# Where the memory's matrices of a hybrid encoder layer are computed: at the start, or in turns with later work

## The chip, the cores and the metric

The kernel runs on one core of a Trainium2 chip. The core has a matrix engine (TensorE, PE in the profile), whose weight loads the profile keeps apart (PEld), a vector engine (VectorE, DVE), a scalar engine (ScalarE, ACT), GpSimd (POOL) and SyncE (SP). Each engine works through its own list of instructions in order; semaphores order the engines against each other. Transfers are started by an instruction on SP, ACT or POOL and run on 16 DMA engines. The metric is device time in microseconds (us) of one execution; smaller is better.

## The reference

One encoder layer over x (2048 tokens of 1024) with a memory of 256 rows:

```python
y = rmsnorm(h, norm_mix_g) @ w_in          # q, k, v, and the conv's value and gate
att = dilated_sliding_attention(q, k, v)   # three patterns, strides 1, 4 and 16
u = a * sigmoid(g)                         # the gated units
conv = silu(layernorm(depthwise_conv(u)))
h = h + concat(att, conv) @ w_out

xq = rmsnorm(h, norm_x_g) @ w_xq           # 4 heads of 256
mn = rmsnorm(mem, norm_mem_g)
xk, xv = mn @ w_xk, mn @ w_xv
pr = softmax(xq xk^T / 16);  h = h + (pr xv) @ w_xo

h = h + square(relu(rmsnorm(h, norm_mlp_g) @ w_up)) @ w_down
return rmsnorm(h, norm_final_g)
```

The cross attention's weights depend on the memory alone. The kernel therefore works out two products per head once, ahead of their use: a score matrix w_xq xk^T (called `pa` in PSUM, `ea` when evicted, `ascr` in DRAM) and a back matrix xv w_xo (`pb`, `eb`, `bscr`).

## The kernel before, in words

The program is one long stream of PE work. Generators stand for the parts; `weave` advances several by given rates, and `pinned` keeps a part's instructions behind what was emitted before them on one engine. What is left open is placed by a scheduler, so the order on each engine is not just that of the code. `ps(kind, ...)` takes a PSUM bank of a kind in turn; `banks` says which banks a kind has, and it is changed between stages.

Products that need float32 accuracy are made of three matmuls on high and low parts (`mm3`, L263 to L266): high by high, low by high, high by low. A weight arrives as `raw`, ACT copies its high part, and DVE or POOL subtracts to get the low one (`wsplit2` L252, `scaled_split` L219).

The stages, in the profile's time:

1. *Start, 0 to 107 us* (`setup0` L148, `setup`, `memory` L414, `xprep` L388). `memory` transposes the memory rows (`mt`), projects the keys with w_xk (`proj` L463: 8 groups of 24 matmuls, `pxk`), transposes w_xq (`turned_wq` L481: 16 groups of 4 transposes, `xqt`, each evicted by an ACT copy and a DVE subtraction) and computes the 16 score groups of 12 matmuls (`pa`, L505 on). It takes turns with `xprep(0)` and `xprep(1)`: squares on ACT for the norm, transposes `xt`, and the high and low parts `xh` (ACT) and `xl` (POOL) of the first 1024 tokens, 512 at a time.
2. *Gated units and projections, 107 to about 455 us*: `pipeline` L604 runs `glu` L624 (two units of 24 matmuls per 512 tokens and 128 channels) for tokens 0 to 1023, then `lin_qk` and `lin_v`; `xprep(2)` and `xprep(3)` lie beside it. The first gated matmul is the first `lin`.
3. *Far stretch, about 455 to 700 us*: attention with stride 16 (`att_far` L983, 124 steps), woven with a filler L1241: the gated units of the later 1024 tokens in turn with `values` L517, which projects the values with w_xv (`pxv`, 8 groups of 24 matmuls) and makes the back matrices (`pb`, 16 groups of 6 matmuls of 512 columns, evicted by ACT at L577).
4. *The rest*: `post` L1453 for four groups of 512 tokens, which begins with `load_cat` L1318, 14 transfers on SP that bring the operand `cath`, `catl` of w_out, and its matmuls `o`; then cross attention and the MLP.

Of the kernel before, what the change touches and what calls it, by code (L numbers as in the profile page):

```python
# [47 lines left out]
def hybrid_layer(ctx, tc, A, out):  # L48
# [16 lines left out]
    banks = {"mm": (0, 1, 2), "a": (3, 4), "b": (5, 6), "c": (7,), "mem": "b"}  # L65
# [17 lines left out]
    def pinned(gen, *names):  # L83

        while True:
            with ExitStack() as st:
                after(st, *names)
                if next(gen, st) is st:
                    return
            yield  # L90

# [27 lines left out]
    vscr = dr.tile([2, KC, P, NMEM], F32R, name="vscr")  # L119
# [28 lines left out]
    def setup0():  # L148
        mvec = t2("mvec", F32, (8, P))
        dma(mvec, A["norm_mem_g"][0].rearrange("(k p) -> k p", p=P))  # L150
        pm = ps("c", "pmvec")
        PE.transpose(pm[:, 0:8], mvec, ident[0:8, 0:8])
        ACT.copy(gm, pm[:, 0:8])

    def setup():
# [7 lines left out]
        dma(vecs[GV["final"]:GV["final"] + 8, :], A["norm_final_g"].rearrange("(k p) -> k p", p=P))  # L163
        dma(cwn[0:CW, :], A["conv_w"][0])
# [197 lines left out]
    def load_nat(sp, src, name, bufs=10, q=None):  # L362
# [9 lines left out]
    def sumsq(sp, t, ss, j, n):  # L372

        for e in range(2):
            q = sp.tile([P, 512], BF16, tag="junk", name="junk", bufs=1)
            ACT.activation(q, t[e], AF.Square, accum_out=ss[:, n * e + j:n * e + j + 1])
# [11 lines left out]
    def xprep(sp, n):  # L388
        xtiles(n)
        nat = [load_nat(sp, A["x"][0, 512 * n + P * j:512 * n + P * (j + 1), :], f"xn{n}_{j}", q=nc.gpsimd if n else None) for j in range(4)]  # L390
# [6 lines left out]
        for k in range(KC):  # L397
# [8 lines left out]
            ACT.copy(XH_[k, n], xv)  # L406
# [7 lines left out]
    def memory(sp, mp):  # L414

        def mpool(part, i, n, name, shape, dtype=F32R):
            return mp.tile(list(shape), dtype, tag=f"m{n}{part}{i}", name=name)

        nat = [load_nat(sp, A["mem"][0, P * j:P * (j + 1), :], f"mn{j}") for j in range(2)]
        mh, ml = ([mpool(q, i, 3, f"m{q}{i}", (P, 4, NMEM)) for i in range(2)] for q in "hl")  # L420
        for k2 in range(KC // 2):
            pt = ps("b", f"mt{k2}")
# [4 lines left out]
            for e in range(2):  # L427
# [4 lines left out]
                DVE.scalar_tensor_tensor(lv, src, gain("mem", k), f(hv), op0=ALU.mult, op1=ALU.subtract)  # L432
        for i, t in enumerate((*mh, *ml)):
            dma(f(mscr[i]), f(t), nc.gpsimd)
        r = rstd_nat(sp, nat, "m")
        rb = ps("c", "rbm")
        bcast_rows(rb, r, 2)
        DVE.tensor_copy(rmem[:, 0:2], r[:, 0:2])
        rbm = sp.tile([P, 2, NMEM], F32, tag="rbm", name="rbm")
        for q in range(2):  # L440
            ACT.activation(rbm[:, q], rb[:, 0:NMEM], AF.Copy, scale=-1.0 / 16.0)
        yield
        cnt = [0]

        def wtiles(name, shape=(P, 8, P)):
            i = cnt[0]
            cnt[0] += 1
            if i % 5 < 2:
                raw = wp.tile(list(shape), F32, tag="raw", name=f"mraw_{name}", bufs=2)
            else:  # L450
                raw = lp.tile(list(shape), F32, tag="lraw", name=f"mraw_{name}", bufs=3)
            if i % 3 < 2:
                return [raw] + [wp.tile(list(shape), F32R, tag=t, name=f"m{t}_{name}", bufs=2) for t in ("whi", "wlo")]
            return [raw] + [mpool(q, 0, 2, f"m{q}_{name}", shape) for q in "hl"]

        def split(src, name, shape=(P, 8, P)):
            raw, hi, lo = wtiles(name, shape)
            dma(raw, src)
            ACT.copy(hi, raw)
            DVE.tensor_tensor(lo, raw, f(hi), op=ALU.subtract)  # L460
            return hi, lo

        def proj(w, name, th, tl):  # L463

            for j in range(KC):
                wh, wl = split(wcols(w, j * P), f"{name}{j}")
                pt = ps("mm", f"p{name}{j}")[:, 0:256]
                for k in range(KC):
                    mm3(pt, wh[:, k, :], wl[:, k, :], mh[k // 4][:, k % 4, :], ml[k // 4][:, k % 4, :],
                        k == 0, k == KC - 1)  # L470
                hv, lv = th[j // 4][:, j % 4, :], tl[j // 4][:, j % 4, :]
                ACT.copy(hv, pt)
                DVE.tensor_tensor(lv, pt, f(hv), op=ALU.subtract)
                yield

        def ttiles(name):
            return [[mpool(q, 2 + i, 3, f"t{q}{name}{i}", (P, 4, NMEM)) for i in range(2)] for q in "hl"]

        th, tl = ttiles("k")
        yield from proj(w_xk, "xk", th, tl)  # L480
        def turned_wq(h):  # L481
            wt = []
            for e in range(2):
                j = 2 * h + e
                raw, whi, wlo = wtiles(f"xq{j}")
                dma(raw, wcols(w_xq, j * P))
                for g in range(2):
                    pt = ps("b", f"xqt{j}{g}")
                    for i in range(4):
                        PE.transpose(pt[:, i * P:(i + 1) * P], raw[:, 4 * g + i, :], ident)  # L490
# [1447 lines left out]
```

## Time and profile before

| what | us |
|---|---|
| median of 3 runs (2831.89, 2821.95, 2821.16) | 2821.95 |
| the profiled execution's own time | 2819.71 |
| its span, first to last instruction | 2817.9 |
| PE busy | 2701.2 |
| DVE, ACT, POOL busy | 1893.7, 1271.2, 510.1 |
| mean granted TensorE clock | .983 |

The profiled execution is one run with a profile taken. Its span leaves out 1.8 us around the first and the last instruction. Busy times overlap between engines and between neighbouring matmuls: a busy PE can still be waiting inside its pipeline, so the prediction counts matmuls by the distance from one start to the next. A row of a group reads: line, engine, operation, output and input names, shapes, count, busy time, mean ns of one, and after the last bar the idle time of the engine ahead of them with what ended it. A row of the timeline reads: start, duration, engine, line, names, and in brackets the idle time before and its releaser.

### The profile page before, as it was taken

To read this page: it belongs to the slowest core of one execution; us is meant where nothing else is said; L and a number is where in the kernel's file an instruction comes from. 1 tells how busy PE (TensorE), PEld (TensorE's weight loads), DVE (VectorE), ACT (ScalarE), POOL (GpSimd) and SP (SyncE) were. 2 spreads that over 40 slices of the span, in tenths; PEclk is the share of its full clock that TensorE was granted. 3 is DMA by queue.
4 is the path that set the end of the run, shared out by engine and by line. 5 is a ranking of instruction groups with operands and counts; after the bars stand their busy time and mean duration, and the time that the engine had idled before them with its cause. 6 is when DMAs were issued, how large, how long until landed. Compare 5 with 4: busy or idle time off the path is not lost.

```text
span 2817.9 us, 40543 instructions
## 1 busy us (share of the span) xinstructions
PE 2701.2 (96%) x14783; PEld 2083.1 (74%) x14783; DVE 1893.7 (67%) x3475; ACT 1271.2 (45%) x2172; POOL 510.1 (18%) x700
## 2 busy tenths in 40 slices
PE   7899999898799999999999999999999999999998
PEld 7554445666677887787878788878887788878877
DVE  5456872665588875667987478766475786666665
ACT  5564322766344333434554443454344444444435
POOL 3346421232002122300111201121010121200000
PEclk8999999999899999999999999999999999999999
DMA  8875555696635666767467866774544554584553
GB/s 283 245 192 135 123 140 162 178 240 187 207 108 172 207 212 222 235 219 219 126 188 222 258 203 213 234 237 139 172 127 131 176 194 154 183 292 155 166 183 105
DMA packets 495135, 531.47 MB, mean 189 GB/s; under 512 B 81253, under 2 KB 371673, under 8 KB 494936
## 3 DMA queue, kind: packets, MB, share of 16 engines
q1 hardware_dynamic: 467528, 440.27, 52.3%
q0 software_dynamic: 25680, 85.38, 8.3%
q10 hardware_dynamic: 1728, 3.24, 0.3%
q8 instruction: 116, 1.90, 0.3%
q14 instruction: 83, 0.68, 0.1%
HBM read 382.36 MB, written 146.42 MB: 188 GB/s over the span
## 4 chain that ended last, share of the span: by engine, by line
PE 69%; DMA 9%; issue 8%; DVE 7%; ACT 3%; POOL 2%; SPq 1%; POOLq 0%; ACTq 0%; DVEq 0%
PE b L1636 7%; PE dn L264 4%; PE dn L265 4%; PE dn L266 4%; PE up L264 3%; PE up L266 3%; PE up L265 3%; PE lin L264 3%; PE lin L265 3%; PE lin L266 3%; PE pt L940 2%; PE s L1133 2%; PE xs L264 1%; PE xs L266 1%; PE xs L265 1%
## 5 line engine op out<-in xcount | busy, mean ns | idle before, releaser
L281 DVE SCALAR_TENSOR_TENSOR cacc<-cu,cwu,cacc 128x512 f32<-128x512 f32 x480 | 390.8, 816 | 6.3
L264 PE MATMUL dn<-hhh,whi_d 128*128 128x512 f32 x512 | 201.7, 404 | 4.3 <-ACT hhh L1473 2.6
L264 PE MATMUL up<-mh,whi_u 128*128 128x512 f32 x512 | 203.9, 398 | 0.0
L934 ACT ACTIVATE sm<-sm,o 128x256 f32<-128x256 f32 (+1 forms) x384 | 160.0, 466 | 96.7 <-DVE o L933 96.3
L265 PE MATMUL dn<-hhl,whi_d 128*128 128x512 f32 x512 | 199.8, 393 | 0.8 <-DVE hhl L1474 0.8
L266 PE MATMUL up<-mh,wlo_u 128*128 128x512 f32 x512 | 200.0, 391 | 0.0
L265 PE MATMUL up<-ml,whi_u 128*128 128x512 f32 x512 | 199.7, 390 | 0.0
L266 PE MATMUL dn<-hhh,wlo_d 128*128 128x512 f32 x512 | 198.8, 391 | 0.0
L933 DVE CUSTOM_DVE_ANT_0 sm<-s,mask 128x256 f32<-128x256 f32 (+1 forms) x384 | 127.2, 374 | 61.3 <-PE s L1133 35.1
L944 DVE TENSOR_TENSOR pl<-pt,ph 128x512 f16<-128x512 f32 x160 | 109.3, 685 | 56.6 <-ACT ph L943 56.4
L1488 DVE TENSOR_TENSOR h<-h,dn 128x512 f32<-128x512 f32 x128 | 86.3, 683 | 70.9 <-PE dn L266 70.4
L943 ACT CAST ph<-pt 128x512 f16<-128x512 f32 x160 | 92.2, 577 | 85.6 <-PE pt L940 85.3
L242 POOL TENSOR_TENSOR nr<-st_v,mhalf 128x4 f32<-128x4 f32 x12 | 13.5, 1125 | 627.8 <-DVE st_v L238 627.8
L264 PE MATMUL o<-cath,whi_o 128*128 128x512 f32 x256 | 103.6, 406 | 12.3 <-DMA cath<-cath 10.8
L264 PEld LDWEIGHTS dn<-hhh,whi_d 128*128 128x128 f32 x512 | 95.4, 188 | 23.3 <-ACT hhh L1473 3.7
L266 PEld LDWEIGHTS up<-mh,wlo_u 128*128 128x128 f32 x512 | 96.1, 188 | 20.4
L266 PEld LDWEIGHTS dn<-hhh,wlo_d 128*128 128x128 f32 x512 | 96.2, 188 | 20.2
L265 PEld LDWEIGHTS dn<-hhl,whi_d 128*128 128x128 f32 x512 | 96.3, 188 | 19.3 <-DVE hhl L1474 1.5
L940 PE MATMUL pt<-ident,sm 128*128 128x128 f32 x640 | 100.9, 277 | 9.8 <-DVE pl L944 3.6
L265 PEld LDWEIGHTS up<-ml,whi_u 128*128 128x128 f32 x512 | 96.3, 188 | 18.7
L264 PEld LDWEIGHTS up<-mh,whi_u 128*128 128x128 f32 x512 | 96.2, 188 | 18.6
L264 PE MATMUL x<-pth,whi_b 128*128 128x512 f32 x256 | 100.3, 397 | 2.4 <-ACT xp L1394 1.4
(598 smaller groups left out, 7934.4 us busy)
## 6 DMA issues: line engine op xcount, KB each, us to landing
raw_u<-in_w_up_dram SPq DMA_DIRECT2D x64, 512.0 KB
raw_d<-in_w_down_dram SPq DMA_DIRECT2D x64, 512.0 KB
k<-kscr SPq DMA_DIRECT2D x32, 640.0 KB
raw_o<-in_w_out_dram SPq DMA_DIRECT2D x32, 512.0 KB
raw_a<-ascr SPq DMA_DIRECT2D x32, 512.0 KB
raw_b<-bscr SPq DMA_DIRECT2D x32, 512.0 KB
lou<-wlo_u POOLq DMA_DIRECT2D x32, 512.0 KB, 5.6
lod<-wlo_d POOLq DMA_DIRECT2D x32, 512.0 KB, 5.6
```

Source lines behind the costliest of these rows:

```text
L264: PE.matmul(o, lh, rh, start=first, stop=False)
L265: PE.matmul(o, lh, rl, start=False, stop=False)
L266: last["pe"] = PE.matmul(o, ll, rh, start=False, stop=end)
L281: DVE.scalar_tensor_tensor(acc, u[:, t:t + 512], cwu[:, c, t:t + 1], acc, op0=ALU.mult, op1=ALU.add)
L933: last["dve"] = DVE.tensor_tensor_reduce(dst, so, mask[:, 256 * m:256 * m + nk], 1.0, 3e38, ALU.add, ALU.min, mn)
L934: last["act"] = ACT.activation(dst, dst, AF.Exp, bias=mn, scale=-1.0)
L940: last["pe"] = PE.transpose(pt[:, j, :], sm[:, j, :], ident)
L943: ACT.copy(ph, pt)
L944: DVE.tensor_tensor(pl, pt, ph, op=ALU.subtract)
L1133: last["pe"] = PE.matmul(o, q_[x][:, qs], kv, start=x == 0, stop=x == 1)
L1488: last["dve"] = DVE.tensor_tensor(hs[m], hs[m], pt, op=ALU.add)
L1636: PE.matmul(o, w[i][:, k, :], Y[b][q][k], start=first and k + x == 0, stop=k == 3 and x == 2, skip_group_check=not first)
```

## The change

- `memory` keeps the norm and the transposes of the memory, comes after the preparation of all tokens, and stores its result (`mscr`).
- A function `glu_first` runs the first pair of gated units as soon as the first 512 tokens are there. The loads of the second 512 tokens go through SP instead of POOL, and the small gain vectors are loaded on ACT's queue instead of SP's.
- A class `Matrices` does everything else in 32 items: 8 projections with w_xk and 8 with w_xv, the turning of w_xq and the score groups, 8 pieces of w_xo for the back matrices. The first 24 are woven with the later gated units in the far stretch (rate 1.6 instead of 1.14, 30 steps ahead instead of 38). Keys take the way of the values, by `pscr` in DRAM.
- The back matrices come after the far stretch, behind the loads of w_out's operand (`load_cat`, taken out of `post`). Their evictions have two buffers (`ve`) instead of eight (`t2`), and their stores and those of the score matrices go out on POOL's queue instead of SP's.

```diff
@@ start block
-        setup0()
-        mp = pool("mem", stack=st)
-        mg = memory(sp, mp)
-        next(mg)
-        next(mg)
         setup()
-        run([mg, chain(xprep(sp, 0), xprep(sp, 1))], (1, 1))
-        banks.update(mm=(0, 1, 2, 5), sq=(6,))
+        pair = glu_first(0, (0, 1))
+        x0, x1 = xprep(sp, 0), xprep(sp, 1)
...
+        drain(x0)
+        for _ in range(3):
+            behind("x0_7", pair)
...
-        units = [u for c in range(4) for u in glu(c, early01)]
+        units = [pair] + [u for c in range(1, 4) for u in glu(c, early01)]
...
+        def hook():
+            ready["gated"] = pipeline(*(u for c in range(4) for u in glu(c, (2, 3), True)))
+            next(ready["gated"])
+            ready["mats"] = Matrices()
...
+        weave(islice(steps, 6), (x1, 1.4))
+        drain(x1)
+        later = pinned(chain(xprep(sp, 2), xprep(sp, 3), memory(sp)), "x1_7")
@@ setup, xprep
-            dma(vecs[GV[key]:GV[key] + v.shape[0], :], v)
+            dma(vecs[GV[key]:GV[key] + v.shape[0], :], v, nc.scalar)
...
-... q=nc.gpsimd if n else None) for j in range(4)]
+... q=nc.gpsimd if n > 1 else None) for j in range(4)]
@@ class Matrices (new)
+        def proj(self, i):
...
+            self.load(i + 2)
+            wh, wl = self.ring.pop(i)
+            pt = ps("mm", f"px{x}{j}")[:, 0:NMEM]
+            for k in range(KC):
+                mm3(pt, wh[:, k, :], wl[:, k, :], mq[k // 4][:, k % 4, :], mq[2 + k // 4][:, k % 4, :],
+                    k == 0, k == KC - 1)
...
+            for q in range(2):
+                dma(f(pscr[x][q, j]), f(t[q]), nc.gpsimd)
...
+        def turn(self, h):
...
+                for g in range(2):
+                    pt = ps("mm", f"xqt{i}{g}")
+                    for x in range(4):
+                        PE.transpose(pt[:, x * P:(x + 1) * P], raw[:, 4 * g + x, :], ident)
...
+        def back(self, i):
+            h, nh = divmod(i - 24, 2)
+            self.load(i + 2)
+            wh, wl = self.ring.pop(i)
+            vt = self.vt
+            for mc in range(2):
+                ms = slice(mc * P, (mc + 1) * P)
+                pt = ps("mm", f"pb{h}{nh}{mc}")
+                for e in range(2):
+                    mm3(pt, vt[h][:, 0, e, ms], vt[h][:, 1, e, ms], wh[:, e], wl[:, e], e == 0, e == 1)
+                if mc == 0:
+                    self.split(i + 1)
+                ev = f(self.pl.tile([P, 512], F32R, tag="ve", name=f"eb{h}{mc}{nh}", bufs=2))
+                ACT.activation(ev, pt, AF.Copy, scale=rmem[:, mc:mc + 1])
+                dma(bscr[4 * nh:4 * nh + 4, :, 2 * h + mc, :].rearrange("m p c -> p m c"),
+                    ev.rearrange("p (m c) -> p m c", c=P), nc.gpsimd)
+                yield
@@ far stretch
         def filler():
-            yield from islice(vals, 2)
-            for g in range(16):
+            for i in range(0, 16, 2):
                 yield from islice(gated, 8)
-                yield from islice(vals, 4 if g < 8 else 2)
+                if i == 0:
+                    mats.norms()
+                yield from mats.proj(i)
+                yield from mats.proj(i + 1)
+            for h in range(XH):
+                yield from mats.turn(h)
+                yield from islice(gated, 8)
+                yield from mats.score(h)
+            mats.split(24)
             yield from gated
-            yield from vals
-            yield from pipeline(ahead(0), ahead(1))
...
-        weave(islice(first, 74), (rest, 1.14))
+        weave(islice(first, 74), (rest, 1.6))
         drain(rest)
-    lin.close()
+        lin.close()
+        zp = pool("post_z")
+        dense = ExitStack()
+        xp_ = pool("post_x", stack=dense)
+        load_cat(0, 0)
+        load_cat(0, 1)
+
+        def backs():
+            for i in range(24, 32):
+                yield from mats.back(i)
+            yield from pipeline(ahead(0), ahead(1))
+
+        drain(pinned(backs(), "pe"))
@@ post
-        if p == 0:
-            load_cat(0, 0)
-            load_cat(0, 1)
```

On PE at the start, before, around the first gated matmul: the last score group, the token transposes `xt`, and then the first `lin`, about 500 rows into PE's list.

```order
L265 MATMUL pa_1394<-tlk_441,mwhi_xq_1229 128x256
L266 MATMUL pa_1394<-thk_439,mwlo_xq_1230 128x256
L208 MATMUL sqs_g_1451<-sqv_g_1449,small 128x1
L400 MATMUL xt_7_1434<-ident,xn_0_1_1038 128x128
...
L264 LDWEIGHTS lwhi_g_1458
L264 MATMUL lin<-xh_0_542,lwhi_g_1458 128x512
```

The same place after; the first `lin` is in PE's row 23, and of the first tokens only the first transposes stand ahead of it.

```order
L249 MATMUL pgain<-ident,gtop 128x128
L207 MATMUL sqs_g_476<-sqv_g_474,small 128x1
L249 MATMUL rb_466<-ident,rsx_457 128x128 x4
L400 MATMUL xt_2_512<-ident,xn_0_0_396 128x128
...
L263 LDWEIGHTS lwhi_g_483
L263 MATMUL lin<-xh_0_388,lwhi_g_483 128x512
L264 LDWEIGHTS lwhi_g_483
L264 MATMUL lin<-xl_0_389,lwhi_g_483 128x512
```

What moved: all `pxk`, `xqt` and `pa` matmuls are gone from ahead of the first gated unit.

On SP at the end of the far stretch, before. `bscr<-eb` are the stores of back matrices, `raw_o` pieces of w_out, and the last row is the first of the 14 operand loads.

```order
L57 DMA bscr<-eb_7704 128x4x128
L57 DMA cath_96<-cth_7658 128x512
L57 DMA bscr<-eb_7714 128x4x128
L57 DMA catl_104<-ctl_7659 128x512
L57 DMA raw_o_8015<-in_w_out_dram 128x8x128
L57 DMA uscr_73<-u_3_7881 128x512
L57 DMA bscr<-eb_7901 128x4x128
L57 DMA bscr<-eb_7935 128x4x128
L57 DMA raw_o_8285<-in_w_out_dram 128x8x128
L57 DMA ld_8166<-oscr_2_93 128x4x132
L57 DMA cath_7972<-cath_98 128x512
```

The same place after: the last two of the 14 operand loads, then the raw loads of the last four pieces of w_xo.

```order
L57 DMA cath_7778<-cath_96 128x512
L57 DMA catl_7779<-catl_104 128x512
L57 DMA raw_m_7838<-in_w_xo_dram 128x2x512
L57 DMA raw_m_7864<-in_w_xo_dram 128x2x512
L57 DMA ld_8187<-oscr_2_93 128x4x132
L57 DMA raw_m_7890<-in_w_xo_dram 128x2x512
L57 DMA raw_m_7916<-in_w_xo_dram 128x2x512
L57 DMA raw_o_7986<-in_w_out_dram 128x8x128
L57 DMA raw_o_7992<-in_w_out_dram 128x8x128
```

What moved: the stores of back matrices have left SP, and four loads that back matrices need stand behind the operand loads.

On ACT at the evictions of back matrices, before, with the semaphores that each row waits for (DMAHW are transfers of SP or ACT, DMASW of POOL).

```order
L577 ACTIVATE eb_7901<-pb_7894,rmem 128x512 [waits DMAHW5_49,PE_49]
L943 CAST ph<-pt 128x512 [waits PE_49,Activation_49]
L1012 COPY o_72_7743<-opt_7913 128x4x65 [waits DMASW0_49,PE_49]
L577 ACTIVATE eb_7935<-pb_7928,rmem 128x512 [waits DMAHW6_49,PE_49]
L255 CAST whi_o_7946<-raw_o_7944 128x1024 [waits DMAHW7_49]
L943 CAST ph<-pt 128x512 [waits PE_49,Activation_49]
```

The same after:

```order
L562 ACTIVATE eb_7799<-pb_7788,rmem 128x512 [waits PE_49]
L562 ACTIVATE eb_7809<-pb_7802,rmem 128x512 [waits PE_49]
L254 CAST whi_m_7821<-raw_m_7786 128x1024 [waits DMAHW0_49]
L254 CAST whi_m_7847<-raw_m_7812 128x1024 [waits DMAHW1_49,PE_49]
L562 ACTIVATE eb_7825<-pb_7814,rmem 128x512 [waits DMASW7_49,Activation_49]
L562 ACTIVATE eb_7835<-pb_7828,rmem 128x512 [waits DMASW0_49,Activation_49]
L254 CAST whi_m_7873<-raw_m_7838 128x1024 [waits DMAHW5_49,DVE_49,PE_49]
L562 ACTIVATE eb_7851<-pb_7840,rmem 128x512 [waits DMASW1_49,Activation_49]
```

What moved: from the third on, an eviction waits for a transfer of POOL's queue, and the split of the first late piece (`raw_m_7838`) stands ahead of the fifth.

More of the change, by code (lines that the diff above doesn't have):

```diff
@@ L90, in pinned, with behind @@
             yield
+    def behind(name, gen):
+        with ExitStack() as st:
+            after(st, name)
+            next(gen)
     def weave(main, *sides):
@@ L147, in hybrid_layer @@
     lin = ExitStack()
[L148 to L153, printed above, removed]
     def setup():
@@ L582, in run @@
-    def run(gens, steps):
-        live = list(zip(gens, steps))
-        while live:
-            for g in list(live):
-                for _ in range(g[1]):
-                    if next(g[0], live) is live:
-                        live.remove(g)
-                        break
+                e3 = ev.rearrange("p (q m) -> p q m", q=2)
+                DVE.tensor_tensor(e3, pt.rearrange("p (q m) -> p q m", q=2),
+                                  self.rbm.unsqueeze(1).to_broadcast([P, 2, NMEM]), op=ALU.mult)
```

308 lines of the change are left out of this document (149 added, 159 removed).

## The prediction

> **What bounds the kernel now.** I read the page's busy times first, then the table of windows cut at the stages that the change touches, then the groups and the waits inside each of these windows. All times are of the profiled execution unless the text says otherwise.
>
> ```profile
> PE 2701.2 (96%) x14783; PEld 2083.1 (74%) x14783; DVE 1893.7 (67%) x3475; ACT 1271.2 (45%) x2172; POOL 510.1 (18%) x700
> 0.00:107.00 107.00, 80.01 (x555) 75.15 (x556) 63.86 (x133) 58.23 (x125) 34.65 (x46) 0.87 0.93 284
> 107.00:455.00 348.00, 345.51 (x1647) 162.59 (x1646) 210.75 (x303) 134.21 (x205) 137.01 (x149) 1.00 0.56 148
> 455.00:700.00 245.00, 223.38 (x2038) 167.40 (x2037) 135.86 (x520) 155.71 (x346) 65.03 (x93) 0.96 0.76 205
> 700.00:712.00 12.00, 1.24 (x5) 0.62 (x3) 1.76 (x2) 1.71 (x3) 0.89 (x1) 0.64 0.83 217
> ```
>
> In each window the columns are its length and the busy time of PE, weight loads, DVE, ACT and POOL, then the granted clock, the DMA share and GB/s. PE is the bound at 96%. The change computes the same matrices, so PE's work is conserved, and only PE time lost to idleness or a low clock can be gained or given back. The stretch from 760 us on is not touched, and 107 to 455 us has 2.5 us to give. That leaves three places: the start, the far stretch (455 to 700) and the seam behind it.
>
> **The start.** A busy PE here includes waiting inside overlapping matmuls, so I count work by spacing at full clock.
>
> ```profile
> L264 PE MATMUL pxk<-mh,mwhi_xk 128*128 128x256 f32 x48 | 15.5, 329 | 2.2 <-ACT mwhi_xk L459 1.7 <-ACT mh L431 0.5
> L264 PE MATMUL pa<-thk,mh_xq 128*128 128x256 f32 x24 | 7.7, 325 | 0.8 <-ACT mh_xq L492 0.8
> L400 PE MATMUL xt<-ident,xn 128*128 128x128 f32 x70 | 12.1, 293 | 11.8 <-DVE xv L405 7.8 <-DMA xn<-in_x_dram 2.8 <-issue 1.2
> L490 PE MATMUL xqt<-ident,mraw_xq 128*128 128x128 f32 x64 | 10.9, 301 | 2.0 <-issue 2.0
> 37.22 0.28 PE L264 MATMUL pxk<-mh,mwhi_xk 128*128 128x256 f32 x1
> 37.34 0.28 PE L265 MATMUL pxk<-ml,mwhi_xk 128*128 128x256 f32 x1
> 81.06 0.44 PE xqt L490 x4
> 107.03 0.63 PE L264 MATMUL lin<-xh,lwhi_g 128*128 128x512 f16 x1
> 109.99 0.38 PE L266 MATMUL lin<-xh,lwlo_g 128*128 128x512 f16 x1
> 110.21 0.38 PE L264 MATMUL lin<-xh,lwhi_g 128*128 128x512 f16 x1
> ```
>
> The first two rows are the first and the last of twelve groups of 256-column matmuls, 384 in all (8 projections of 24 for the keys, 16 score groups of 12). At .118 us apart (37.22 to 37.34) they are 45.3 us. Some 160 transposes at .44/4 = .11 are 17.6. The work up to the first gated matmul at 107.03 is thus about 63 us, and 107 − 63 = 44 us are lost.
>
> **The start after.** The projection and score matmuls (45.3 us) and the turning of w_xq (7 us) leave; the gated units follow the first tokens at once. PE's loss is now what the preparation of x takes. It goes by these rows:
>
> ```profile
> 3.51 0.75 SPq L57 DMA_DIRECT2D vecs<-in_norm_mix_g_dram  x1
> 8.63 0.23 SPq L57 DMA_DIRECT2D cwn<-in_conv_w_dram  x1
> 0.74 1.28 ACT L153 ACT_TABLE_LOAD   x1 [0.74 <-PEq L1921]
> 3.84 0.63 ACT L376 ACTIVATE junk<-mn 128x512 bf16<-128x512 f32 x1 [1.15 <-DMA mn<-in_mem_dram]
> 4.60 0.63 ACT L376 ACTIVATE junk<-mn 128x512 bf16<-128x512 f32 x1
> L220 ACT ACTIVATE lraw_g<-lraw_g,wscl 128x1024 f32<-128x1024 f32 x4 | 4.6, 1141 | 2.7 <-DVE wscl L189 2.7
> L221 ACT CAST lwhi_g<-lraw_g 128x1024 f16<-128x1024 f32 x4 | 4.1, 1036 | 0.1
> L407 POOL TENSOR_TENSOR xl<-xv,xh 128x512 f16<-128x512 f32 x23 | 26.5, 1158 | 42.5 <-ACT xh L406 42.5
> L222 POOL TENSOR_TENSOR lwlo_a<-lraw_a,lwhi_a 128x1024 f16<-128x1024 f32 x4 | 8.5, 2133 | 4.1 <-ACT lwhi_a L221 3.0 <-issue 1.0
> L57 POOL DMA_DIRECT2D xn<-in_x_dram x14 | 7.6, 550 | 7.4 <-PE xt L400 7.4
> ```
>
> ACT now issues the eight vector loads that took SP 3.51 to 8.86 = 5.35 us: .74 + 5.35 = 6.1. With the table load (1.28) it is free at 7.4. Eight squares at .76 (4.60 − 3.84) end at 13.8, the rstd chain (about 2.5, my estimate, bounds 1.5 to 4) at 16.3; scale 1.14, cast 1.04 and the row broadcast with the first xh about 1.2 give the first gated matmul at 20 to 21. Then POOL is the slow engine: from 19.4, two low parts of weights (2 × 2.13), 16 xl × 1.16 = 18.6, one rstd step about 1, and 16 loads of later tokens to issue × .55 = 8.8 are 32.7, so the second 512 tokens are complete at 52. By 55 PE has done 96 gated matmuls × .2155 (109.99 to 110.21 gives .22) = 20.7, 64 transposes = 7, and 1.3 of the small ones: 29 of 55. It loses 26 there and some 2 in the next units while ACT is full: 28. **Start: 44 − 28 = +16** (bounds +8, if the gated units wait for POOL's xl in each step to 65 us, and +21, if the loads of later tokens slide behind).
>
> **The far stretch.** Lost now: idle 245 − 223.4 = 21.6, and clock (1−.96) × 245 = 9.8. The waits in it that are longest in total:
>
> ```profile
> PE opt L950 <- DVE pl L944: 7.3, 10, 1.6
> PE pt L940 <- DVE pl L944: 3.6, 2, 3.0
> 90.44 0.48 ACT mwhi_xq L492
> 90.94 0.46 DVE mwlo_xq L493
> ```
>
> The columns are us in total, times, longest. The work that fills between 124 attention steps was 82.8 (384 gated matmuls × .2155) + 22.7 (192 value matmuls × .118) + 21.8 (96 matmuls of 512 columns × .227, as from 700.19 to 700.43 below) = 127 us. Now it is 82.8 + 45.3 + 22.7 + 7 = 158: 1.27 instead of 1.02 us for each step. Twelve waits × .25 = 3 fall, and a quarter to a third of the clock's 9.8 with them, 3. Against this, each xqt group ends in an ACT copy (.48) and a DVE subtraction (.46) on one of two banks, .94 against .44 of PE: (.44+.94)/2 − .44 = .25 × 16 = 4. ACT and DVE are 64% and 55% busy here (155.7 and 135.9 of 245), and I have no row of these groups beside attention: from −26 (a full wait of 1 us for each of 32 groups, less the 6) to +12 (half of the idle time and nothing new). I take the near one, since attention's own steps stand between the groups: **far: +2**.
>
> **The seam.** Now PE ends at 700.43 and waits for w_out's operand:
>
> ```profile
> 700.19 0.40 PE L265 MATMUL pb<-wlo_mv,mvv 128*128 128x512 f32 x1
> 700.43 0.40 PE L266 MATMUL pb<-whi_mv,mvv 128*128 128x512 f32 x1
> 711.58 0.76 PE L264 MATMUL o<-cath,whi_o 128*128 128x512 f32 x1 [10.76 <-DMA cath<-cath]
> 717.17 0.39 PE L266 MATMUL o<-cath,wlo_o 128*128 128x512 f32 x1
> 706.48 0.81 SPq L57 DMA_DIRECT2D cath<-cath  x2
> 714.67 0.32 SPq L57 DMA_DIRECT2D catl<-catl  x1
> L577 ACT ACTIVATE eb<-pb,rmem x16: 666/688/692, 595.7 to 700.9; 128x512 f32<-128x512 f32 x16
> vscr<-veh POOLq DMA_DIRECT2D x8, 128.0 KB, 4.6
> oscr<-o POOLq DMA_DIRECT2D x20, 264.0 KB, 6.2
> rb<-r POOLq DMA_DIRECT2D x48, 256.0 KB, 2.3
> ```
>
> The loss is 10.8 + .4 + the cold clock after it (12 matmuls from 711.58 to 717.40 in 5.8 less .4 instead of 12 × .227 = 2.7): 14 us. After, 16 groups of six matmuls (L577's 16 evictions) fill it with 16 × 6 × .227 = 21.8 us of work. Were they free to run, all 14 would be gained. Two waits hold them. First, on SP the raw loads of the last four w_xo pieces now stand behind the 14 operand loads, whose issue takes 706.48 to 714.99 = 8.5 us; the first of these pieces lands some 15.5 us after the stretch ends (8.5, one more .4, and the 5.2 below, with 1.4 until the memory comes free), and ACT's split of it stands ahead of the fifth eviction. Second, an eviction has two buffers where it had eight, and its store moves from SP to POOL's queue: eviction n+2 waits until store n has landed. POOL's stores of this size in this neighbourhood land in 4.6 (128 KB) to 6.2 us (264 KB), so two groups take .69 + .2 + 5.2 = 6.1 us where PE has 2 × 1.36 = 2.7 to do. The rest is 15.5 + 1.0 (cast) + .7 + 4 × 6.1 + 3 = 45 us for 21.8 of work: 23 lost instead of 14. **Seam: −9.** At the 2.3 us of the rb row it is 4 × 3.2 + 20 = 33, 11 lost: +3. If the operand loads beside them make the stores half as slow again (8.5, my estimate from the 5.2), it is 58: −22.
>
> The Trainium skill's page "DMA: Bandwidth & Descriptors", section "Anatomy of one DMA — SWDGE (gpsimd) path", gives a transfer issued by GpSimd as 2.0 us plus bytes at 436 GB/s, 2.6 for 256 KB. By it the seam would be about +2 and the kernel near 2802. The rb row agrees with it, the oscr row (6.2 us for 264 KB) does not.
>
> **Edits at nothing.** The keys now go to DRAM and come back as the values did: 16 more stores and, with the score matrices moved from SP, another 16 for POOL to issue, 32 × .55 = 18 us of POOL, which is busy 65 of 245 in this stretch; the cover is that emptiness. Were it gone, the first score group would wait for the last store of v and its gather, a landing each, about 10 us; the turning of the first head's w_xq and eight gated steps (8 × 3 × .2155 = 5) stand between. The memory's norm and transposes, now after the tokens, and its four stores lie beside the 107 to 455 stretch's gated units, POOL being busy 137 of 348 there. SP loses the vector loads (5.35 us) ahead of the first weights and takes the second tokens' loads; PE doesn't wait for these before POOL's chain is done.
>
> **Sum:** 16 + 2 − 9 = 9. The span 2817.9 becomes 2809; the profiled execution of 2819.71 becomes 2810.7. It lies 2.24 under the median of 2821.95, so the forecast for the median is **2813 us**.
>
> **The rivals.** *B, stores are quick.* The stores land in 2.3 us, as rb does late in the kernel when little else moves; for it speaks that PE stands and attention is idle at the seam, against it that the operand loads are moving at the same time (217 GB/s in 700 to 712). 16 + 2 + 2.5 = 20.5: **2801**. A low clock would take part of that.
>
> ```profile
> 705.00:710.00 5.00, 0.00 (x0) 0.00 (x0) 0.00 (x0) 0.00 (x0) 0.00 (x0) 0.50 0.86 218
> ```
>
> The row shows .50 after five idle us. The Trainium skill ("TensorE: Matmul & The Clock Gate", section "HAM oscillation — how this bites in real kernels") says that idle gaps over about 3.4 us throw PE back to half clock. In the forecast PE idles 3.4 us in each cycle of 6.1, so half-speed groups would hide inside the cycle; by rival B's cycle of 3.2 they would cost 16 × 1.3 = 20 and take its gain away.
>
> *C, slower.* The bank is the mechanism, in the far stretch: each of the 16 xqt and 16 score groups finds ACT or DVE at an attention step and PE, in order, waits 1 us for it. 16 − 26 − 9 = −19: **2841**. With w the mean wait of 32 groups, the kernel is slower than before from 32 w = 13, so w = .41 us, and by over 0.5% from w = .85.
>
> *D, the change doesn't do what it says at the start.* The xl chain on POOL holds the gated units as it held the transposes (42.5 us idle to xh shows POOL was not the limit there, against it), and the gain is 2: 2 + 2 − 9 = −5: **2827**.
>
> **How the numbers follow.** Half a per cent, 14 us, is about what a measurement of this kernel can tell from no change: 2807.8 and 2836.1. The forecast has .40 (its terms' bounds put .08 of it under 2807.8 and .02 over 2836.1); B .28 (.26 faster, .02 same); C .20 (.16 slower, .04 same); D .12 (.10 same, .02 slower). That makes .34 faster, .46 same, .20 slower. The range runs from 2797, four us under B, to 2838, which leaves out the upper half of C and the far ends.
>
> **What would show it.** First gated matmul at 20 to 22 us, and at least 48 of these matmuls before 40 us: start right; after 40 us, D. PE's idle time on the fill line of xqt or the score groups over 13 us between 420 and 700: C. At the seam, L562 (the eviction's line after) waiting for POOL's store, pairs of groups 6 us apart, and 40 to 50 us from the last attention step to the first w_out matmul: forecast; under 35: B. A first wait there for the raw piece of w_xo of about 5 us shows the SP queue. The forecast is wrong if the time from 760 us on differs by more than a few us, or if the 107 to 455 stretch, which had no slack, has gaps.

## The result: 48 us slower

The changed kernel takes 2869.14 us against 2821.55 us, a ratio of 1.0167 (95% interval 1.0138 to 1.0196). The forecast was 2813, with a range to 2838. PE's busy time is nearly the same (2709.2 against 2701.2 us), so most of the 49 us of span are PE time lost. The windows of the changed kernel, cut at its own stages (columns as in the prediction):

```profile
0.00:107.00 107.00, 64.43 (x289) 34.89 (x290) 43.88 (x110) 62.74 (x138) 46.13 (x54) 0.89 0.78 232
107.00:455.00 348.00, 333.16 (x1608) 162.55 (x1607) 210.62 (x286) 117.31 (x168) 127.81 (x144) 0.99 0.56 149
455.00:722.00 267.00, 233.33 (x2249) 186.33 (x2249) 155.03 (x551) 152.59 (x344) 80.46 (x119) 0.96 0.70 195
722.00:768.00 46.00, 28.98 (x96) 21.07 (x95) 9.69 (x12) 18.39 (x26) 11.42 (x15) 0.81 0.76 241
850.00:2867.00 2017.00, 1976.86 (x10147) 1618.90 (x10145) 1426.26 (x2407) 889.61 (x1443) 268.71 (x409) 1.00 0.59 190
```

To compare stages although work has moved between them, I count the work done up to each moment (each recorded matmul at the spacing of its shape at full clock) and call the rest of the time lost. The table gives the loss between fixed amounts of work: 80 us of work is about the end of the start, 390 the end of the projections, 592 the first back matrix after, 640 a point behind the seam.

| kernel | to 80 | 80–390 | 390–592 | 592–640 | 640–2600 |
|---|---|---|---|---|---|
| before | 44.6 | 2.3 | 37.0 | 29.6 | 68.2 |
| after | 57.3 | 23.6 | 48.0 | 40.1 | 62.4 |
| zeros late | 51.7 | 24.6 | 45.5 | 36.9 | 65.0 |
| eight buffers | 58.5 | 23.1 | 48.8 | 34.1 | 64.8 |
| buffers, pieces on ACT | 56.3 | 22.4 | 49.8 | 33.1 | 62.5 |
| ld on POOL | 58.5 | 24.2 | 30.6 | 40.5 | 61.9 |
| tokens evenly | 58.3 | 18.3 | 48.9 | 37.7 | 60.6 |
| plain start | 57.7 | 17.5 | 46.0 | 38.6 | 59.3 |
| plain start, zeros, ld | 56.7 | 17.4 | 30.3 | 41.6 | 63.7 |
| four edits | 47.5 | 23.3 | 39.5 | 36.5 | 68.7 |
| three stages | 47.8 | 20.5 | 26.0 | 38.8 | 65.1 |

The change costs 13 us at the start, 21 beside the projections, 11 in the far stretch and 10 at the seam. The last column is work that the edits do not touch; it moves by up to 10 us from one profiled run to another. Of the edits tried alone, only the one of attention's loads ("ld on POOL") has an interval clear of the changed kernel's, so gains below 10 us are read from the stage that the edit touches.

**Start.** The waits of PE to 120 us, the stop itself in PE's timeline, what DVE waited for, and SP's timeline at that place, all of the changed kernel:

```profile
PE xt L400 <- DVE xv L405: 15.7, 3, 13.8
24.54 0.63 PE L263 MATMUL lin<-xh,lwhi_g 128*128 128x512 f16 x1
46.35 1.94 PE L400 MATMUL xt<-ident,xn 128*128 128x128 f32 x8 [13.80 <-DVE xv L405]
44.86 0.69 DVE L402 COPY xts<-xt 128x512 f32<-128x512 f32 x1 [15.41 <-DMA xscr<-xts]
18.36 3.02 SPq L57 DMA_DIRECT2D vtok<-zrow  x2
21.42 13.20 SPq L57 DMA_DIRECT2D uscr<-zero  x8
37.74 0.38 SPq L57 DMA_DIRECT2D xscr<-xts  x1
26.00:33.00 7.00, 5.37 (x19) 2.60 (x18) 2.10 (x3) 4.61 (x12) 5.88 (x8) 1.00 0.91 129
DMA packets 543, 0.90 MB, mean 129 GB/s; under 512 B 182, under 2 KB 182, under 8 KB 543
40.00:50.00 10.00, 3.65 (x13) 2.52 (x14) 4.49 (x8) 2.28 (x5) 3.06 (x5) 0.50 0.86 289
```

The first gated matmul comes at 24.5, not at 107, and then PE stops for 14 us: the transposed tokens are copied out by DVE through three buffers whose stores to DRAM wait on SP behind ten zero stores, 16 us of issuing. Two of these (`vtok<-zrow`) write 520 KB each, in packets of 2080 bytes; the eight others (`uscr<-zero`) have 7.5 or 8.5 KB, in packets of 60 or 68 bytes. From 26 to 33 us the DMA engines are 91% busy and move only 129 GB/s (the row of packets is of this window). In the trace the packets of the large two fill 77% of the engines' time there and the small ones under 2%; the small stores are issued slowly (4.7 us for each of the first two) while the large ones run. The clock then falls to .50.

The kernel before has the same ten stores in another order: the eight small ones at 30 us, issued in 5.4 us, the two large ones at 69 us. Behind those the engines are as busy for as few bytes, and PE, which has the turning of w_xq and the score groups to do, doesn't stop:

```profile
70.00:80.00 10.00, 10.00 (x90) 10.00 (x89) 8.63 (x16) 3.50 (x7) 1.17 (x1) 1.00 0.93 138
```

**Projections.** Here no wait is long. These are the largest between 107 and 455 us, 12.4 of the 14.8 us that PE idles there; the clock of .99 is up to another 3:

```profile
PE lin L263 <- DVE rope_qr L833: 4.4, 3, 1.5
PE pmvec L421 <- DMA mvec<-in_norm_mem_g_dram: 3.5, 1, 3.5
PE vbc L249 <- DVE raw_v L696: 2.8, 1, 2.8
PE pxk L264 <- DMA mvm<-mscr: 1.7, 2, 1.2
```

**Far stretch.** The longest single wait of PE and of DVE, then SP's timeline and DVE's next instruction:

```profile
PE xqt L522 <- issue: 11.9, 1, 11.9
DVE csm L1066 <- DMA ld<-oscr: 11.6, 1, 11.6
599.63 0.88 SPq L57 DMA_DIRECT2D k<-kscr  x1
605.21 0.54 SPq L57 DMA_DIRECT2D ld<-oscr  x1
615.00 0.17 DVE L1066 TENSOR_TENSOR csm<-ld 128x8 f32<-128x8 f32 x1 [11.61 <-DMA ld<-oscr]
```

DVE stands from 603 to 615 for a load that was issued at 605.2, behind the next heads' operands. PE then stops at a turned group, since its bank is emptied by DVE: the profile names no releaser there, but DVE's subtraction for these groups starts at 615.6 and PE at 616.4.

**Seam.** The evictions of back matrices and their stores, then PE's two longest waits and ACT's for the first piece of w_xo behind the operand loads:

```profile
L562 ACT ACTIVATE eb<-pb,rmem x16: 678/687/689, 723.4 to 771.7; 128x512 f32<-128x512 f32 x16
L57 POOL DMA_DIRECT2D bscr<-eb x16: 752/752/764, 724.4 to 772.7; - x16
DMA to landing us min/median/max: 2.7/4.6/8.1
733.26 0.80 PE L263 MATMUL pb<-whi_m,vt 128*128 128x512 f32 x1 [5.72 <-ACT eb L562]
744.26 0.79 PE L263 MATMUL pb<-whi_m,vt 128*128 128x512 f32 x1 [6.63 <-ACT eb L562]
742.58 1.04 ACT L254 CAST whi_m<-raw_m 128x1024 fp32r<-128x1024 f32 x1 [7.99 <-DMA raw_m<-in_w_xo_dram]
```

Both waits of the prediction are there: evictions wait for stores, and the piece lands at 742.5.

### The profile page after: what moved, and what is told of

The parts are those of the page before. It is cut to its first block, busy times and chain, and to the rows that moved or that the text cites. A ratio compares the mean times of both kernels' runs of the same rounds, so it can differ in the third digit from the quotient of the medians.

```text
span 2867.3 us, 40621 instructions
## 1 busy us (share of the span) xinstructions
PE 2709.2 (94%) x14783; PEld 2082.4 (73%) x14783; DVE 1902.0 (66%) x3475; ACT 1274.5 (44%) x2171; POOL 538.1 (19%) x744
## 4 chain that ended last, share of the span: by engine, by line
PE 65%; issue 10%; DVE 8%; DMA 8%; ACT 3%; POOL 3%; SPq 2%; POOLq 0%; ACTq 0%; DVEq 0%
PE b L1670 7%; PE dn L263 4%; PE dn L264 4%; PE dn L265 4%; PE up L263 3%; PE up L265 3%; PE up L264 3%; PE pt L962 2%; SPq L57 2%; DVE cacc L280 2%; PE s L1155 2%; PE x L264 1%; PE x L263 1%; PE x L265 1%; PE lin L263 1%
## 5 line engine op out<-in xcount | busy, mean ns | idle before, releaser
L280 DVE SCALAR_TENSOR_TENSOR cacc<-cu,cwu,cacc 128x512 f32<-128x512 f32 x480 | 396.8, 828 | 6.4
L265 PEld LDWEIGHTS up<-mh,wlo_u 128*128 128x128 f32 x512 | 96.1, 188 | 20.5
L263 PE MATMUL xs<-whi_a,yh 128*128 128x512 f32 x256 | 102.3, 401 | 0.0
```

The source lines that it names most:

```text
L263: PE.matmul(o, lh, rh, start=first, stop=False)
L265: last["pe"] = PE.matmul(o, ll, rh, start=False, stop=end)
L280: DVE.scalar_tensor_tensor(acc, u[:, t:t + 512], cwu[:, c, t:t + 1], acc, op0=ALU.mult, op1=ALU.add)
```

## The experiments

Each is the changed kernel with the edit shown, unless it is said to start from the kernel before. Expectations are quoted as put down ahead of the run.

**Zero stores late.**

`xs1_7` is the last store of the second tokens, on SP.

```diff
-            dma(xscr[k][:, 512 * n:512 * (n + 1)], xt)
+            last[f"xs{n}_{k}"] = nc.sync.dma_start(xscr[k][:, 512 * n:512 * (n + 1)], xt)
...
-    edges()
+    with ExitStack() as late:
+        after(late, "xs1_7")
+        edges()
```

> The changed kernel with its ten zero stores (two to the padded v in DRAM, eight of 15 or 17 columns to the padded conv input) issued on SP behind the stores of the second 512 tokens instead of ahead of the third store of the first. Theory: PE's stop of 14 us at 32 to 46 us is DVE waiting for a buffer whose store stands behind these zeros; it goes, the first 107 us lose about 43 us instead of 57, and the kernel comes to about 2855 (14 less than 2869). Rival: the DMA engines are full with 4 MB of tokens and 2 MB of weights, the store lands late in any order; a stop of 8 us or more stays and the kernel is within 5 us of 2869.

2860.82 us, ratio to before 1.0146 (1.0127 to 1.0166). The 14 us stop is gone, so the zeros were its cause; all ten were moved, so this run alone does not tell the large from the small. But the loss to 80 us of work falls by 6, not 14. Counted in smaller steps, the loss to 15 us of work falls from 51 to 37, the whole 14; between 20 and 50 us of work it is then 13 instead of 5.5. The zero stores now run from 65 to 83 us, and the last row below, at this place, has PE busy for 5.8 of 10 us, the clock at .66 and the engines at 87% for 144 GB/s. The four waits were there before with nearly the same times (4.1, 3.2, 5.2 and 4.4 us in the changed kernel).

```profile
PE pvec L167 <- DMA cwn<-in_conv_w_dram: 5.5, 1, 5.5
PE sqs_g L207 <- ACT sqj_g L202: 3.9, 2, 3.1
PE rb L249 <- DVE rsx L244: 3.6, 3, 1.7
PE lin L264 <- POOL xl L407: 3.2, 5, 1.1
70.00:80.00 10.00, 5.81 (x17) 2.48 (x18) 5.55 (x14) 7.39 (x16) 5.26 (x3) 0.66 0.87 144
```

**Vector loads on POOL** (`nc.scalar` to `nc.gpsimd` at the eight loads).

> The changed kernel with the eight loads of gain vectors on POOL's queue instead of ACT's. Theory of the prediction's sum (ACT's chain sets the first gated matmul, and the issues are 5 us of it): the first gated matmul comes 3 to 5 us earlier than 24.5; the kernel gains 0 to 4 us, since the stop at the zero stores stays. Rival (the landing of the convolution weights behind the tokens' loads sets it): no earlier than 24.

2873.18 us; the first gated matmul is at 24.13. ACT's 5 us of issuing do not set it, and the rival's time holds. In both kernels PE waits over 4 us for what these loads bring (4.1 for the convolution weights after, 4.6 for the gains here), which speaks for their landing; no run changes that.

```profile
24.13 0.63 PE L263 MATMUL lin<-xh,lwhi_g 128*128 128x512 f16 x1
18.95 0.45 PE L249 MATMUL pgain<-ident,gtop 128*128 128x128 f32 x1 [4.60 <-DVE gtop L173]
```

**No hand-made first unit.**

```diff
-        pair = glu_first(0, (0, 1))
...
+        drain(xprep(sp, 0), xprep(sp, 1))
-        units = [pair] + [u for c in range(1, 4) for u in glu(c, early01)]
+        units = [u for c in range(4) for u in glu(c, early01)]
...
+        weave(islice(steps, 15), (later, 1.6), (qks, 1))
```

> The changed kernel with one part undone: no function for the first pair of gated units; both groups of tokens are prepared first in the program, the gated units follow in the ordinary pipeline, and the scheduler may mix them. Theory: the hand-made first unit is worth nothing, since ACT's and POOL's preparation of the second tokens and the low clock set the start either way; first 107 us within 4 us of 57 lost, and with the tokens behind it spread as in the kernel before, the 107 to 455 stretch loses 12 us or less instead of 21.6: 2855 to 2862. Rival (the first unit at once is what keeps the start from being worse): the start loses 62 us or more, the kernel 2868 or above.

2856.46 us, 1.0147 (1.0119 to 1.0175). The scheduler now starts the first unit at 32.6, 8 us later, and the start loses the same (57.7). The first unit at once was worth nothing here; 80 to 390 improves by 6, though not to 12. The edit also spreads the later tokens in another way, so that 6 belongs to both together.

**Later tokens spread evenly.**

```diff
-        weave(islice(steps, 16), (later, 0.25), (qks, 0.25))
-        weave(islice(steps, 11), (later, 2.4), (qks, 0.7))
+        weave(islice(steps, 16), (later, 1.0), (qks, 0.25))
+        weave(islice(steps, 11), (later, 1.3), (qks, 0.7))
```

> The changed kernel with the preparation of the later tokens spread evenly beside the gated units (rates 1.0 and 1.3 per step instead of .25 and 2.4). Theory: the 18 us that PE loses more between 107 and 455 us come from this preparation crowding DVE, ACT and POOL beside the query and key projections; the stage loses 14 us or less instead of 21.6, and the kernel comes to 2858 to 2863. Rival (the waits belong to the memory's norm load and the projections' own evictions): 19 us or more stay, the kernel within 4 us of 2869.

2861.27 us, 1.0145 (1.0117 to 1.0174), with 18.3 instead of 23.6 lost. For the stage neither side is met: crowding is about a quarter of its loss. The wait for the memory's norm load goes with it; those for `rope_qr` (3.6 us) and `raw_v` (3.2) stay.

**Score stores on SP** (`nc.gpsimd` removed at `ascr`).

> The changed kernel with the 16 stores of score matrices back on SP's queue. Theory: on POOL's queue they delay the stores of attention's output behind them (10 us to landing instead of 6), and with them the load that DVE waits for in order, and all that DVE would evict; the 12 us stop of PE at 604 and the 4.5 us one at 690 go, the far stretch loses 35 to 38 us instead of 50, and the kernel comes to about 2855. Rival (two banks for the turned weights, as in the prediction's rival C): the stops at the turned weights stay, as ACT and DVE evict no faster, and the kernel is within 4 us of 2869.

2869.1 us. The theory falls: PE's stop at the turned weights is 8.9 us, and DVE still waits for the same load.

```profile
614.54 0.17 DVE L1066 TENSOR_TENSOR csm<-ld 128x8 f32<-128x8 f32 x1 [8.62 <-DMA ld<-oscr]
```

**Gated steps ahead of the turning** (the two lines exchanged in `filler`).

> The changed kernel with the eight gated steps of each head ahead of its turning of w_xq instead of behind. Theory: at 604 us DVE waits in order for attention's loads (11.6 us), and PE stops because a turned group needs DVE within its two banks and offers only .44 us of work; with gated units there, which need DVE once in 48 matmuls, PE has 5 to 8 us to do, so the 12 us stop becomes 7 or less and the kernel 2861 to 2865. Rival: the stop is the lateness of attention itself, moves with it and stays over 9 us, the kernel within 4 us of 2869.

2871.85 us. DVE still waits 8.0 us ahead of the instruction that reads the load, and PE stops elsewhere (longest waits 7.7 and 5.2 us). This speaks for the load's lateness, and not for what PE has to do beside it; the next run tests it.

```profile
PE opt L972 <- DVE pl L966: 9.0, 5, 5.2
PE pt L962 <- ACT sm L956: 8.7, 2, 7.7
```

**Attention's loads on POOL's queue.**

```diff
             dma(ld[:, i].rearrange("p j h e -> p j (h e)"),
-                oscr[pr][i][...].rearrange("(j p) e -> p j e", p=P))
+                oscr[pr][i][...].rearrange("(j p) e -> p j e", p=P),
+                nc.sync if p else nc.gpsimd)
```

> The changed kernel with the loads of attention's stored outputs (ld, first 512 tokens) on POOL's queue instead of SP's. Theory: at 604 us DVE waits in order for such a load, which is issued at 605.2 behind some 2 MB of other loads on SP and lands at 615; on a queue with little in it the load lands by 608, the 12 us stop of PE becomes 4 or less, the far stretch loses 40 to 44 us instead of 50, and the kernel comes to 2858 to 2862. Rival: the DMA engines themselves are full (99% in the profile at this place), the load lands as late from any queue, and the stop stays over 8 us.

2852.18 us, 1.0111 (1.0095 to 1.0127): 17 us for one line. The loads are issued at 590.9 and 594.9, as soon as attention's stores that they read have landed, and land in 6.2 us; DVE has no wait for them, and the far stretch loses 30.6 instead of 48.0, less than before. The second load lands at 601 instead of 615, most of it by being issued 10 us earlier. From 590 to 597 the engines move 370 GB/s here, so the rival is refuted: with full DMA engines the order on the queue still decided.

```profile
590.93 0.76 POOL L57 DMA_DIRECT2D ld<-oscr  x1 [2.06 <-DMA oscr<-o]
594.95 0.76 POOL L57 DMA_DIRECT2D ld<-oscr  x1 [3.25 <-DMA oscr<-o]
ld<-oscr POOLq DMA_DIRECT2D x2, 264.0 KB, 6.2
PE xqt L522 <- DVE wlo_m L525: 6.1, 5, 1.8
```

The last row is all that is left of PE's waits at the turned weights: the 12 us stop is gone.

**The seam.** Eight buffers (the eight tiles that hold h later), pieces of w_xo on ACT's queue, and both:

```diff
-                ev = f(self.pl.tile([P, 512], F32R, tag="ve", name=f"eb{h}{mc}{nh}", bufs=2))
+                ev = zp.tile([P, 512], F32, tag=f"z{(2 * i + mc) % 8}", name=f"eb{h}{mc}{nh}")
```

```diff
-            dma(raw, src)
+            dma(raw, src, nc.scalar if i >= 26 else None)
```

> The changed kernel with eight buffers for the evicted back matrices instead of two, the stores still on POOL's queue. Theory (the cycle of buffer and store sets the pace, the prediction's second wait): the 46.5 us from the first back matrix to the first w_out matmul become 29 to 33, the kernel about 2854. Rival (the raw pieces of w_xo behind the operand loads on SP set the pace): 41 us or more, the kernel at 2864 or above.

> The changed kernel with the last six pieces of w_xo loaded on ACT's queue, so that they don't stand behind the 14 operand loads on SP; two buffers for evictions as in the change. Theory (buffer cycle): the 46.5 us stay within 3 us, the kernel 2866 to 2870. Rival (order on SP sets the pace): under 40 us, the kernel under 2863.

> The changed kernel with both edits of the seam: eight buffers for the evicted back matrices, and the last six pieces of w_xo loaded on ACT's queue. Each alone gave 0 to 4 us. Theory (two limits of nearly equal length, each hiding the other): together 46.5 us from the first back matrix to the first w_out matmul become 30 or less, and the kernel comes to 2852 to 2856. Rival (a third limit, such as the transfers themselves): 38 us or more, the kernel above 2860.

2865.55, 2871.53 and 2863.13 us. From the first back matrix to the first w_out matmul it takes 41.4, 45.6 and 40.3 us, against 46.5. With eight buffers the rival's time holds, with the pieces on ACT the theory's: alone, neither limit gives much, since the other stands behind it. With buffers enough PE waits 14 us for the piece behind the operand loads (first row). With both edits the rival holds again and a third limit shows: ACT waits 8.3 us in order before it issues a piece (second and third row), until a load issued by SP (`catl`) has landed, and the DMA engines are full at 401 GB/s.

```profile
748.94 0.79 PE L263 MATMUL pb<-whi_m,vt 128*128 128x512 f32 x1 [14.08 <-ACT whi_m L254]
738.62 0.38 ACTq L57 DMA_DIRECT2D raw_m<-in_w_xo_dram  x1
739.05 1.26 ACT L562 ACTIVATE eb<-pb,rmem 128x512 f32<-128x512 f32 x2 [8.30 <-DMA catl<-catl]
732.00:740.00 8.00, 0.68 (x3) 0.24 (x3) 0.00 (x0) 0.95 (x2) 0.00 (x0) 0.68 1.04 401
```

**From the kernel before: half of the back matrices behind the operand loads**, first with their stores on SP, then on POOL. The evictions of this half go to eight tiles (not shown).

```diff
-                yield from islice(vals, 4 if g < 8 else 2)
+                yield from islice(vals, 4 if g < 8 else 2 if g < 12 else 0)
...
+        load_cat(0, 0)
+        load_cat(0, 1)
+        def tail():
+            yield from vals
+            yield from pipeline(ahead(0), ahead(1))
+        drain(pinned(tail(), "pe"))
```

> The kernel before with one part of the change alone: the back matrices of the last four pieces of w_xo (8 of 16 groups, 10.9 us of work) behind the operand loads of w_out, with eight buffers and their stores on SP. Theory (back matrices behind the operand loads are worth what PE idles there, if the buffers last): PE's 10.8 us of idle time at 700 us go except what the pieces on SP hold back, the kernel comes to 2808 to 2813. Rival (the operand loads then hold up the pieces, as in the changed kernel): a stop of 8 us or more inside the back matrices, the kernel 2816 to 2822.

> The kernel before with the back matrices of the last four pieces of w_xo behind the operand loads, and the stores of these back matrices on POOL's queue. With the stores on SP, PE idled 8.9 us for the first piece of w_out (raw_o), whose load stood behind these stores and was issued at 706.8. Theory: issued at 701.5 it lands by 708, PE idles 2 to 4 us, and the kernel comes to 2812 to 2815 against 2819 to 2821 before. Rival (the transfers of the seam need this time in any order): PE idles 7 us or more, no change within 3 us.

2819.01 us (ratio .9996, .9984 to 1.0008) and 2818.74 (.9997, .9988 to 1.0007): no change. PE runs through the back matrices without a stop and then waits for the first piece of w_out instead: 8.7 us with the stores on SP, 9.8 without, although its load is then issued at 699.1 instead of 706.8.

```profile
714.66 0.79 PE L264 MATMUL o<-cath,whi_o 128*128 128x512 f32 x1 [8.70 <-ACT whi_o L255]
713.93 0.79 PE L264 MATMUL o<-cath,whi_o 128*128 128x512 f32 x1 [9.80 <-ACT whi_o L255]
706.00:715.00 9.00, 0.34 (x1) 0.34 (x2) 0.36 (x1) 1.73 (x2) 0.00 (x0) 0.78 1.05 318
700.00:714.00 14.00, 4.20 (x19) 3.03 (x18) 1.32 (x2) 3.80 (x5) 3.10 (x5) 0.80 1.02 324
```

The first and the third row are of the stores on SP, the others of those on POOL. The DMA share is 1.05 and 1.02 while PE waits: in both orders the engines are full, and it looks as if the transfers themselves set the end. No run takes a transfer away to show it.

**From the kernel before: ld on POOL.**

> The kernel before with attention's loads ld (first 512 tokens) on POOL's queue. Theory: the load's place on SP behind the next head pair's operands costs the kernel before little, since DVE reaches it late (2.6 us of waiting in the far stretch, and part of the 10 us around 741); 2812 to 2819 against 2820, a gain of 2 to 8 us. Rival: POOL's queue then delays attention's stores, no change or up to 5 us slower.

2820.97 us (1.0008, .9994 to 1.0021): no change, as the rival had it. The line that gives 17 us after gives nothing before, where DVE waits 2.6 us for this load.

```profile
DVE csm L1044 <- DMA ld<-oscr: 2.6, 1, 2.6
```

**Edits together**: zeros, ld and both seam edits; then one edit in each of three stages (zeros, even tokens, ld); then the plain start with zeros and ld.

> The changed kernel with four edits together: the zero stores behind the second tokens' stores, attention's loads ld on POOL's queue, eight buffers for back matrices, and late pieces of w_xo on ACT's queue. Theory (separate causes in separate stages): the gains add, 8 + 17 + 6 = 31, and the kernel comes to 2836 to 2842; what is then left over the kernel before, about 18 us, lies between 107 and 455 us. Rival (a gain ahead only moves the wait behind): 2845 or more.

> The changed kernel with one edit in each of three stages and the seam as it is: zero stores late, later tokens' preparation spread evenly, attention's loads ld on POOL. Alone they gave 8, 8 and 17 us. Theory (the stages are separate): the gains add, 2869 - 33 = 2836, at most 2840. Rival (what is gained ahead is given back behind, as four edits together gave no more than ld alone): 2846 or more.

> The plain start together with late zero stores and attention's loads ld on POOL. If the gains add, 2830 to 2838; if what is gained ahead is given back, 2845 or more. Either way it stays above the kernel before (2819 to 2821), since the seam keeps its 10 us.

2851.4 us, 2839.69 us (1.0081, 1.0059 to 1.0104) and 2846.94 us. In three stages the gains add: 29 of 33 us. With the four edits they don't: the far stretch loses 39.5, where it loses 30.6 with ld on POOL alone. In that kernel ACT, which needs to issue a piece of w_xo, waits in order behind attention's loads, and PE behind ACT. No run has zeros, ld and buffers without the pieces, so that these waits are the whole difference is argued from their size.

```profile
669.41 0.40 ACT L958 ACTIVATE sm<-sm,o 128x128 f32<-128x128 f32 x1 [9.50 <-DMA v<-vtok]
669.86 0.77 PE L964 MATMUL pt<-ident,sm 128*128 128x128 f32 x2 [6.49 <-ACT sm L958]
```

With the plain start they don't add either: 9.5 us less than the plain start alone, where 25 were expected. By the table ld gives its 16 us there, but the late zeros give the start 1 us (56.7 against 57.7), and 7 us are lost again behind the far stretch, 4 of them in work that no edit touches. So with this start the zero stores are not what holds PE up; what does, no run shows.

No kernel tried beats the kernel before.

## Why the prediction was wrong

- **Start, "44 − 28 = +16": the step that failed first.** It is −13. The 28 was a chain through ACT and POOL; SP was costed only by what it loses. The ten zero stores stand ahead of the token stores when PE has nothing else to do: 14 us. Moving them is worth 6 to 10 us at the start made by hand (51.7, 47.5 and 47.8 instead of 57.3), and 1 us at the plain one. The first gated matmul is at 24.5 instead of 20 to 21; I put that on ACT, and the run with the loads on POOL shows that it isn't ACT's issues. The 28 had no term for the low clock, although the 44 had held it: .87 over the first 107 us before is up to 14 us, .89 after up to 12, part of it while PE stands. With the zeros gone the loss is still 51.7, which I attribute to the many short waits and the clock; no run took these away, so the cause of this rest is open.
- **107 to 455, "has 2.5 us to give", and the edits at nothing.** I read a stage without slack as one that cannot get worse, and covered the memory's norm by POOL's idle time. It lost 21 us more. About 5 to 6 are the bunched preparation; for the other 15 no cause is shown beyond the waits listed.
- **Far, "+2".** It is −11, but not by rival C. By the prediction's own sign C looked met: PE idles 17.6 us at the turned weights, over its 13. But 11.9 of these are one stop that goes with the load's queue; the other waits there are 5.7 us in five, where C needed about 1 us at each of 32 groups. A load on SP that lands at 615 instead of 601 cost 17. I counted new loads and stores as issue time on POOL, and not as a queue ahead of attention's loads.
- **Seam, "−9": right, the closeness with luck.** 46.5 us from the first back matrix to the first w_out matmul, where 45 was worked out; the loss is 10 more than before. Both waits came, but two misses offset each other: the first piece landed 21 us after the stretch's end instead of 15.5, and what follows it took 26 us instead of 29. Stores landed in 2.7 to 8.1 us, median 4.6, where 5.2 was taken. By the Trainium skill's page "DMA: Bandwidth & Descriptors" ("Anatomy of one DMA — SWDGE (gpsimd) path"), 2.0 us plus bytes at 436 GB/s, the estimate for this size is 2.6 us; here only the quickest store comes near it, and the measurement decides. What the prediction missed is that each of its two waits hides the other (5 and .9 us of the 46.5 alone, 6 together), and that the transfers are a third limit just behind.
- **The sum.** It added one stage's gain to others' losses and was wrong by 56: 29 at the start, 21 beside the projections, 13 in the far stretch and 1 at the seam make 64, and the profiled run loses 6 less in the last column. The range was made of bounds on the priced terms alone.

## What to carry to other kernels

Before moving work out of a stage, list what each queue does in that stage while the work covers it: stores and loads that cost nothing behind it can become the bound when it is gone. Where DVE or ACT waits in order for a load, look at what stands ahead of that load on its queue: here moving it to an emptier one gave 17 us, and no reordering of PE's work gave as much. A gap that PE spends on transfers was not filled here by work that brings its own transfers.

## What was not expected of the hardware

Two zero stores of 520 KB, rows of 2080 bytes read from one tile of 16 partitions, kept the DMA engines about 90% busy for some 10 us, at 129 GB/s after, 138 before and 144 with the zeros late. Their packets took 298 ns at the median, those of 2048 bytes beside them 84. The Trainium skill's page "DMA: Bandwidth & Descriptors", section "Specifications", gives 512 bytes as the least transfer for line rate; these rows are four times as long and far from it, so by this figure their length does not explain it, and why they are slow stays open. The 1024 packets of 60 and 68 bytes of the eight small stores, 11 to 12 ns each, took less than 1 us of all 16 engines.

And a load issued by ACT waited 8.3 and 9.5 us for transfers that SP had issued: in the trace ACT waits, ahead of the load, for the semaphore that the load then uses and that an older transfer of SP had used (`catl` in the first case). So moving it off SP did not free it from SP's transfers.
